# State-space stage: the diagonal products as two column tiles of 64 instead of one over 128 columns

## The chip, the cores and the metric

One of the eight cores of a Trainium2 chip runs the kernel. The metric is the device time of one execution in microseconds (us). Three runs of the kernel before gave 2584.29, 2584.89 and 2587.09 us; the median is 2584.89 us.

## The reference

The reference is one layer of a hybrid decoder over 1024 tokens of width 1024: token mixing (stick-breaking attention beside a Mamba-2 state-space branch), cross-attention into 256 memory tokens, and a SwiGLU feed-forward. What matters here is the state-space branch. It has 32 heads of width 64 in 4 groups of 8, and it works on chunks of 128 rows. Within a chunk each head's output has a diagonal term: a lower triangular 128 x 128 matrix (the group's C times B products, times the head's decay) applied to the head's 128 x 64 inputs.

```python
decay = jnp.exp(jnp.where(tril, a_cs[..., :, None] - a_cs[..., None, :], -jnp.inf))
cb = jnp.einsum('bclgn,bcsgn->bcgls', cc, bc)
y_diag = jnp.einsum('bcgls,bcgels,bcsgep->bclgep', cb, decay, xc)
...
return (y_diag + y_off).reshape(b, l, h, p)
```

Here `l` is the output row of the chunk, `s` the input row, `e` the head in its group and `p` the 64 columns of a head.

## The kernel before, in words

The kernel is one long program for five engines, and its stages follow each other: the input projection, the convolution and gates, attention, the state-space stage (from about 1080 to 1437 us of the span), the gated merge, cross-attention, the feed-forward. A scheduler that works from its own estimate of every instruction's duration writes the order on each engine; the text of the kernel gives the dependences, and some hand-set marks that keep one instruction behind another.

The state-space stage works on 32 pairs of a group and a chunk. For each pair it has these steps, which the scheduler lets overlap with those of other pairs:

- `prep` loads the inputs `xs` (128 rows x 512 columns: 8 heads of 64), makes the decay by a product on TensorE (L1048) and an exponential on ScalarE (L1049), and multiplies it by the C times B products on VectorE (L1050). The result is `seg`, 8 matrices of 128 x 128, one for each head, with the input row on the partitions and the output row along the free dimension.
- `states` carries the running state from chunk to chunk (TensorE L104 to L106 into `pst`, GpSimd L1072, VectorE L1073, then a split into a high and a low part, ScalarE L98 and VectorE L101).
- `outp` forms the output. GpSimd starts `y` with the skip term (L1089). The term of the earlier chunks comes from three matmuls into `po`, VectorE L1094 and GpSimd L1095. The diagonal term comes from **8 matmuls into `pd` (L1100)**, one for each head; their weights are `seg` of the head, their moving operand the head's columns of `xs`. VectorE adds `pd` to `y` (L1103) and multiplies by the gate (L1104). ScalarE makes the sum of squares (L1107), and the scaling follows (L1109).
- `flip` turns `y` by four transposes (L1122), and `branch` multiplies it with a weight matrix (the groups `mm<-oth,bw` of L104 to L106, which are most of the stage's matmuls). In the first quarter of the stage, matmuls of the memory's keys and values run between these steps.

The matmuls into `pd` are plain float32, not the rounded float32 kind (`fp32r`) that the others use. A float32 matmul shows as two passes, each with a weight load (engine PEld in the profile) and a matmul (PE): 32 pairs x 8 heads x 2 passes are the 512 records of L1100. The weights are 128 columns wide, so a pass writes all 128 partitions of `pd`. The moving operand is 96 columns and not 64, except for head 0: the loop goes from head 7 down to head 0, and each matmul also writes the 32 columns left of its own, which the next head's matmul writes again. `pd` has one buffer, so a pair's first matmul into it waits for the L1103 of the pair before.

Another matmul of the kernel, L406 at about 45 to 58 us, has weights of 64 columns only and writes partitions 0 to 63; it stands among others with 128.

Of the kernel before, what the change touches and what calls it, by code (L numbers as in the profile page):

```python
# [25 lines left out]
NH, HD = 16, 64  # L26
NG, GH = 4, 8
# [7 lines left out]
def hybrid_block(ctx, tc, a, out, dbg=None):  # L35
    nc = tc.nc
    V, A, G, T = nc.vector, nc.scalar, nc.gpsimd, nc.tensor
# [11 lines left out]
    def mk(pl, shape, dt, tag, bufs=None):  # L49
        uid[0] += 1  # L50
        kw = {} if bufs is None else {"bufs": bufs}
        return pl.tile(shape, dt, tag=tag, name=f"{tag}_{uid[0]}", **kw)
# [50 lines left out]
    def mm3(ps, sh, sl, mh, ml, start, stop):  # L103
        first = T.matmul(ps, sh, mh, start=start, stop=False)  # L104
        T.matmul(ps, sh, ml, start=False, stop=False)  # L105
        T.matmul(ps, sl, mh, start=False, stop=stop)  # L106
        return first
# [42 lines left out]
    def rstd_of(ms):  # L150
        r = mk(stats, [P, 1], F32, "rstd")
        G.tensor_scalar(r, ms, EPS, None, ALU.add)  # L152
        G.tensor_tensor(r, r, mhalf, ALU.pow)
        return r
# [94 lines left out]
    with ExitStack() as pa:  # L249
# [486 lines left out]
        with ExitStack() as p2:  # L736
# [17 lines left out]
            marks = []  # L754
# [174 lines left out]
            for m in range(NM):  # L929
                h, half = m // 2, m % 2  # L930
                hp, r = m // 4, m % 4
# [18 lines left out]
    with ExitStack() as p3:  # L950
# [11 lines left out]
        def bc(t, c, g, n=HD):  # L962
            return t[:, c, g * GH:(g + 1) * GH].unsqueeze(2).to_broadcast([P, GH, n])

        def v3(t, n=HD):
            return t.rearrange("p (h d) -> p h d", d=n)
# [114 lines left out]
        def outp(n):  # L1081
            g, c = divmod(n, NCH)
            d, gd = chk[n], grp[g]
            rows_ = slice(c * P, (c + 1) * P)
            seg, xs = d["seg"], d["xs"]
            zs = mk(t2, [P, HALF], F32, "s2")
            nc.sync.dma_start(zs, zs_d[rows_, g * HALF:(g + 1) * HALF])
            y = mk(t2, [P, HALF], F32, "s2")
            G.tensor_tensor(v3(y), v3(xs), dsk[:, g * GH:(g + 1) * GH].unsqueeze(2).to_broadcast([P, GH, HD]), ALU.mult)  # L1089
            if c > 0:  # L1090
                po = mk(ps, [P, HALF], F32, "po")
                mm3(po, d["ch"], d["cl"], *gd["st", c], True, True)
                yo = mk(t2, [P, HALF], F32, "s2")
                V.tensor_tensor(v3(yo), v3(po), bc(eam, c, g), ALU.mult)  # L1094
                G.tensor_tensor(y, y, yo, ALU.add)  # L1095

            pd = mk(ps, [P, HALF], F32, "pd")
            for h in range(GH - 1, -1, -1):
                hs = slice(max(0, h * HD - 32), (h + 1) * HD)
                ins = T.matmul(pd[:, hs], seg[:, h, :], xs[:, hs], start=True, stop=True)  # L1100
                if h == GH - 1:
                    marks.append(ins)
            V.tensor_tensor(y, y, pd, ALU.add)  # L1103
            V.tensor_tensor(y, y, zs, ALU.mult)  # L1104
            junk = mk(t2, [P, HALF], BF16, "junk", bufs=1)
            ms = mk(stats, [P, 1], F32, "ms")
            A.activation(junk, y, AF.Square, scale=float(HALF) ** -0.5, accum_out=ms)  # L1107

            A.activation(y, y, AF.Copy, scale=rstd_of(ms))  # L1109
            d["y"] = y  # L1110
# [56 lines left out]
        marks = []  # L1167
# [102 lines left out]
        for n in range(-AHEAD, NN + 2):  # L1270
            if AHEAD <= n + AHEAD < NN:
                prep(n + AHEAD)
            mem_work((n + AHEAD) * NQ / MEM_SPAN)
            for l in loads.pop(n, []):
                branch_load(*l)
            if todo and todo[0][0] <= n:
                todo.pop(0)[1]()
            if 0 <= n + 1 < NN:
                states(n + 1)
            mem_work((n + AHEAD + 0.33) * NQ / MEM_SPAN)  # L1280
            if 0 <= n < NN:
                outp(n)
            mem_work((n + AHEAD + 0.67) * NQ / MEM_SPAN)
            if todo and todo[0][0] <= n:
                todo.pop(0)[1]()
            if 0 <= n - 2 < NN:
                flip(n - 2)
                if (n - 2) % 4 == 3:
                    g, c = divmod(n - 2, NCH)
                    fs = list(range(KT)) if c == 3 else list(range(4, KT)) + list(range(4))  # L1290
                    todo += [(n + 2, lambda g=g, hf_=c // 4, f=f: branch(g, hf_, f)) for f in fs]
# [70 lines left out]
    marks = []  # L1362
# [506 lines left out]
```

## Time and profile before

| | |
|---|---|
| time, median of 3 runs | 2584.89 us (2584.29 to 2587.09) |
| profiled execution | span 2585.2 us, from its first to its last instruction (the profile gives no other time of it) |
| granted TensorE clock, mean | 0.990 |
| TensorE matmul / weight load busy | 2493.1 us (96%) / 2061.1 us (80%) |
| VectorE, ScalarE, GpSimd busy | 69%, 44%, 33% |
| the matmuls into `pd` | 512 passes, 1105.8 to 1432.6 us |

PE is TensorE's matmuls and PEld its weight loads, which run beside the matmuls; DVE is VectorE, ACT ScalarE, POOL GpSimd and SP the engine that issues DMAs. A row of the timeline gives the start in us, the duration in us, the engine, the source line, the operation, what it writes and reads, the shapes and how many follow each other; `128*64` or `128*128` ahead of the shapes is rows times columns of the weights in the array. A matmul's record begins when it comes to the head of the array and holds its wait for weights, if there is one.

### The profile page before, as it was taken

The page shows a single profiled execution, that of the slowest core. Times are in us where ns is not written, and L with a number is a line of the kernel's source. Part 1 is how long each engine was busy: PE and PEld are TensorE (multiplying, and loading weights), DVE is VectorE, ACT ScalarE, POOL GpSimd, SP SyncE. Part 2 cuts the span into 40 slices and gives each one's busy share as a digit, 9 for nine tenths or more (in the row PEclk, how much of TensorE's full clock was granted, in tenths as well). Part 3 has the DMA queues.
Part 4 walks back from the last instruction along what each step waited for, and adds up shares of the span by engine and source line. Part 5 has one row for each costly group of instructions (what it writes and reads, how often), then busy time and mean ns, then how long its engine had stood idle before and what let it go on. Part 6 is the DMA issues. An engine that isn't in the chain of part 4 may idle for free. (4 is left out here: it accounts for less than half of the span.)

```text
span 2585.2 us, 32334 instructions
## 1 busy us (share of the span) xinstructions
PE 2493.1 (96%) x11866; PEld 2061.1 (80%) x11866; DVE 1793.6 (69%) x2093; ACT 1130.1 (44%) x2020; POOL 842.2 (33%) x650
## 2 busy tenths in 40 slices
PE   7999999999999999999999999999999999999998
PEld 5788887887888778787888788887787888887876
DVE  7765777776578887687888664416459666666997
ACT  5333455555466655455554312314234333334343
POOL 3221654443111111244655050101114333323762
PEclk9999999999999999989999999999999999999999
DMA  7431433333543443355322462411232232224232
GB/s 245 155 121 58 151 117 103 109 106 91 141 107 98 118 104 90 111 180 175 104 90 81 153 238 74 130 49 50 94 113 70 76 96 74 90 90 163 98 131 98
DMA packets 255272, 293.44 MB, mean 114 GB/s; under 512 B 17024, under 2 KB 175241, under 8 KB 254987
## 3 DMA queue, kind: packets, MB, share of 16 engines
q1 hardware_dynamic: 255114, 291.40, 36.2%
q8 instruction: 93, 1.52, 0.2%
q14 instruction: 65, 0.52, 0.1%
HBM read 200.10 MB, written 74.45 MB: 106 GB/s over the span
## 5 line engine op out<-in xcount | busy, mean ns | idle before, releaser
L861 DVE TENSOR_TENSOR_SCAN n<-n,mask 128x128 f32<-128x128 f32 (+7 forms) x128 | 189.6, 1506 | 23.5 <-ACT n L860 22.2
L101 DVE TENSOR_TENSOR sw<-sf,sw 128x512 fp32r<-128x512 f32 x150 | 129.0, 872 | 67.0 <-ACT sw L98 66.7
L183 POOL TENSOR_TENSOR sf<-wr,wr 128x512 f32<-128x512 f32 x38 | 59.3, 1560 | 277.8 <-DMA wr<-in_w_gu_dram 138.3
L878 ACT ACTIVATE wth<-tr,mone 128x512 fp32r<-128x512 f32 x192 | 110.6, 584 | 83.0 <-PE tr L875 82.3
L98 ACT ACTIVATE sw<-sf 128x512 fp32r<-128x512 f32 x150 | 92.0, 626 | 109.1 <-PE mm L217 94.0
L879 DVE SCALAR_TENSOR_TENSOR wtl<-tr,wth 128x512 fp32r<-128x512 f32 x192 | 99.7, 544 | 50.6 <-ACT wth L878 50.6
L101 DVE TENSOR_TENSOR sw<-wr,sw 128x512 fp32r<-128x512 f32 x113 | 107.7, 955 | 27.6 <-ACT sw L98 27.5
L217 PE MATMUL mm<-h,sw 128*128 128x512 f32 x320 | 124.8, 391 | 1.8 <-DVE sw L101 1.8
L215 PE MATMUL mm<-h,sw 128*128 128x512 f32 x320 | 122.6, 391 | 2.9 <-ACT h L98 2.3
L216 PE MATMUL mm<-h,sw 128*128 128x512 f32 x320 | 125.1, 391 | 0.0
L104 PE MATMUL mm<-oth,bw 128*128 128x512 f32 (+1 forms) x320 | 122.5, 383 | 2.3 <-DVE a L1159 2.0
L98 ACT ACTIVATE sw<-wr 128x512 fp32r<-128x512 f32 x113 | 70.7, 628 | 120.9 <-PE mm L217 120.8
L106 PE MATMUL mm<-oth,bw 128*128 128x512 f32 (+1 forms) x320 | 120.0, 375 | 1.5 <-DVE bw L1146 1.5
L105 PE MATMUL mm<-otl,bw 128*128 128x512 f32 (+1 forms) x320 | 119.1, 372 | 0.0
L663 DVE SCALAR_TENSOR_TENSOR b<-b,prmT,b 128x1023 f32<-128x1023 f32 (+2 forms) x72 | 108.6, 1511 | 10.7 <-ACT b L661 10.0
L94 POOL TENSOR_SCALAR v<-va 128x512 fp32r<-128x512 f32 x16 | 20.6, 1291 | 285.4 <-PE av L888 165.8
L860 ACT ACTIVATE n<-sc 128x512 f32<-128x512 f32 (+1 forms) x192 | 88.6, 494 | 45.6 <-PE tr L875 28.8
L152 POOL TENSOR_SCALAR rstd<-ms 128x1 f32<-128x1 f32 x74 | 27.9, 376 | 242.3 <-ACT x L1380 111.5
L104 PE MATMUL p<-bw,h 128*128 128x512 f32 x256 | 99.4, 393 | 3.3 <-DVE x L1382 2.4
L106 PE MATMUL p<-bw,h 128*128 128x512 f32 x256 | 100.8, 394 | 0.0
L105 PE MATMUL p<-bw,h 128*128 128x512 f32 x256 | 100.4, 392 | 0.0
L185 POOL TENSOR_TENSOR sf<-wr 128x512 f32<-128x512 f32 x38 | 63.4, 1667 | 110.2 <-DVE sw L101 110.2
(607 smaller groups left out, 8033.1 us busy)
## 6 DMA issues: line engine op xcount, KB each, us to landing
wr<-in_w_gu_dram SPq DMA_DIRECT2D x80, 256.0 KB
wr<-in_w_in_dram SPq DMA_DIRECT2D x36, 512.0 KB
zr<-in_w_in_dram SPq DMA_DIRECT2D x28, 512.0 KB
gu_d<-t SPq DMA_DIRECT2D x44, 256.0 KB
wraw<-in_w_in_dram SPq DMA_DIRECT2D x20, 512.0 KB
zs_d<-zo SPq DMA_DIRECT2D x32, 256.0 KB
xs_d<-b SPq DMA_DIRECT2D x32, 256.0 KB
kl<-gt SPq DMA_DIRECT2D x64, 128.0 KB
```

The costliest lines, as they stand in the source:

```text
L98: A.activation(o, i, AF.Copy)
L101: eng.tensor_tensor(o, i, hi.bitcast(F32), ALU.subtract)
L104: first = T.matmul(ps, sh, mh, start=start, stop=False)
L105: T.matmul(ps, sh, ml, start=False, stop=False)
L106: T.matmul(ps, sl, mh, start=False, stop=stop)
L215: T.matmul(ps, w[0][:, k, :], bh, start=first and k == 0, stop=False, skip_group_check=True)
L216: T.matmul(ps, w[0][:, k, :], bl, start=False, stop=False, skip_group_check=True)
L217: ins = T.matmul(ps, w[1][:, k, :], bh, start=False, stop=last and k == 3, skip_group_check=True)
L663: V.scalar_tensor_tensor(acc[:, sh:], y[:, :S - sh], cw(3 - sh, f), acc[:, sh:], ALU.mult, ALU.add)
L861: V.tensor_tensor_scan(nt[:, 0:L][:, ::-1], nt[:, 0:L][:, ::-1], mask[:, S - L:][:, ::-1], 1.0, ALU.mult, ALU.max)
L878: A.activation(wh[:, t0 * P:], pt[:, t0 * P:], AF.Identity, bias=mone)
L879: V.scalar_tensor_tensor(wl[:, t0 * P:], pt[:, t0 * P:], -1.0, wh[:, t0 * P:].bitcast(F32), ALU.add, ALU.subtract)
```

## The change

The diagonal product of a head is cut in two along the output rows. One matmul has the weights for rows 0 to 63 (64 of the 128 columns of the head's `seg`) and writes partitions 0 to 63 of `pd`; a second has those for rows 64 to 127 and writes partitions 64 to 127. In the array these are two column tiles, of 128 rows by 64 columns each, at columns 0 and 64. Both have the same moving operand, the head's own 64 columns; the 32 columns more are gone. There are 16 matmuls for each pair in place of 8, or 1024 passes in place of 512, with weight loads of 64 columns in place of 128. The mark that keeps other work behind the first of these matmuls is set on the first half of head 7.

```diff
             pd = mk(ps, [P, HALF], F32, "pd")
             for h in range(GH - 1, -1, -1):
-                hs = slice(max(0, h * HD - 32), (h + 1) * HD)
-                ins = T.matmul(pd[:, hs], seg[:, h, :], xs[:, hs], start=True, stop=True)
-                if h == GH - 1:
-                    marks.append(ins)
+                hs = slice(h * HD, (h + 1) * HD)
+                for j in range(2):
+                    r = slice(j * HD, (j + 1) * HD)
+                    ins = T.matmul(pd[r, hs], seg[:, h, r], xs[:, hs], start=True, stop=True)
+                    if h == GH - 1 and j == 0:
+                        marks.append(ins)
             V.tensor_tensor(y, y, pd, ALU.add)
```

## The prediction

> **What bounds the kernel now.** I read the page's first lines, then the stage in which the changed matmuls stand, by stretches, then what TensorE waits for in it.
>
> ```profile
> span 2585.2 us, 32334 instructions
> PE 2493.1 (96%) x11866; PEld 2061.1 (80%) x11866; DVE 1793.6 (69%) x2093; ACT 1130.1 (44%) x2020; POOL 842.2 (33%) x650
> ```
>
> ```profile
> core 0: us, PE busy (x) PEld busy (x) DVE busy (x) ACT busy (x) POOL busy (x), PEclk, DMA share, GB/s
> 1105.00:1437.00 332.00, 320.48 (x1808) 274.59 (x1807) 273.25 (x333) 173.06 (x327) 174.00 (x167) 0.98 0.39 119
> ```
>
> ```profile
> PE pd L1100 <- DVE s L1103: 2.5, 2, 1.8
> PE dec L1048 <- ACT s L1049: 2.2, 3, 1.3
> PE dec L1048 <- DVE cb L1025: 1.6, 1, 1.6
> ```
>
> The second fence is the stretch of 332 us that holds all the changed matmuls. PE is busy for 320.5 of it, 97%; VectorE comes next with 273 us, 82%. The third fence has PE's longest waits there (us in total, times, longest): 2.5 us is the largest. So TensorE bounds this stage, and work taken off it or put on it changes the time nearly one for one, until VectorE's order catches up. A busy PE is not one at its peak, though; a short matmul may be waiting for its weights. So the next view is one run of the changed matmuls, first the matmuls and then the weight loads:
>
> ```profile
> 1207.54 0.40 PE L106 MATMUL mm<-oth,bw 128*128 128x512 f32 x1
> 1207.77 1.89 PE L1100 MATMUL pd<-s,s 128*128 128x96 f32 x16
> 1209.47 0.47 PE L104 MATMUL mm<-oth,bw 128*128 128x512 f32 x1
> 1209.79 0.39 PE L105 MATMUL mm<-otl,bw 128*128 128x512 f32 x1
> ```
>
> ```profile
> 1207.54 1.99 PEld L1100 LDWEIGHTS pd<-s,s 128*128 128x128 f32 x16
> 1209.45 0.19 PEld L104 LDWEIGHTS mm<-oth,bw 128*128 128x128 f32 x1
> 1209.56 0.19 PEld L105 LDWEIGHTS mm<-otl,bw 128*128 128x128 f32 x1
> ```
>
> The first load of the run starts at 1207.54, under the wide matmul ahead of it, and the second when the first pass starts, at 1207.77. From there to the load of the next wide matmul, at 1209.45, lie 15 more: 1.68 us / 15 = 0.112 us each, and the next pair of loads (1209.45, 1209.56) stands 0.11 apart too. Each load begins as soon as the one before is done. Is it the load that sets this pace, or the matmul? The durations say, in ns (minimum, median, maximum); the first row is the whole of L1100, the second the first pass of this run:
>
> ```profile
> L1100 PE MATMUL pd<-s,s x512: 218/275/422, 1105.8 to 1432.6; 128*128 128x96 f32 x149, 128*128 128x64 f32 x22
> L1100 PE MATMUL pd<-s,s x1: 244/244/244, 1207.8 to 1207.8; 128*128 128x96 f32 x1
> L1100 PEld LDWEIGHTS pd<-s,s x2: 187/188/188, 1207.5 to 1207.8; 128*128 128x128 f32 x2
> ```
>
> The first pass, whose weights lay ready, took 244 ns with 96 columns; the shortest of all, 218, I take as one with 64. The 26 ns between them over 32 columns are 0.81 ns a column: 64 columns stream in 52 ns, 96 in 78. Both are less than 112. **The runs are bound by their weight loads**, and the 32 columns that fall away are worth nothing.
>
> **The change part by part.** *The loads.* What does a load of 64 columns cost? L406 has such loads, among matmuls that start 0.23 us apart as here (rows below):
>
> ```profile
> L406 PEld LDWEIGHTS pdt<-b11h,wds x4: 133/134/135, 45.7 to 49.3; 128*64 128x64 f32 x4
> ```
>
> 134 ns against 187 to 188 for 128 columns: 53.5 ns less for 64 columns less. Of the load's record the part that sets the pace is 112 ns, so a load of 64 columns should allow a pace of 112 - 53.5 = 58 ns. The matmul of 64 columns streams in 52 ns, so the load still sets the pace. Half the load, twice as many: that is the whole trade, and it comes out slightly worse, since the fixed 5 ns a load (112 - 2 x 53.5) is paid twice.
>
> How many? The order in which the two built programs hold PE's instructions shows the passes of the 32 pairs in 47 runs before (some pairs are split by other matmuls) and in 50 after. In each run the first load lies under the wide matmul ahead, and the load of the wide matmul behind it, 112 ns, is paid in its place. Before: 512 x 0.112 = 57.3 us, whichever load it is. After: (1024 - 50) x 0.058 = 56.5 us, and 50 x 0.112 = 5.6 us for the wide loads, together 62.1 us. The difference is **+4.8 us**; at PE's 97% of the stretch, +4.6.
>
> The pace of two halves in turn, at columns 0 and 64, is the one price that no row shows: L406 uses the left half alone. Bounds from the nearest rows: 29 ns a pass if the two halves load wholly side by side (two passes each 58 ns), 112 ns if a narrow pass keeps the pace of a wide one. I take 58, since the rows for both halves of the pair (load 134, stream 52) give it without a new mechanism.
>
> *The passage between widths.* Ahead of and behind each run the array changes from tiles of 128 columns to tiles of 64 and back, 100 times. L406 does so before:
>
> ```profile
> 45.67 0.40 PE L216 MATMUL pv<-vl,b11h 128*128 128x512 f32 x1
> 45.90 0.39 PE L406 MATMUL pdt<-b11h,wds 128*64 128x512 f32 x1
> 46.13 0.39 PE L217 MATMUL pv<-vh,b11l 128*128 128x512 f32 x1
> 46.36 0.40 PE L215 MATMUL pv<-vh,b11h 128*128 128x512 f32 x1
> ```
>
> Starts are 0.23 us apart in all three steps, into the narrow tile, out of it, and between two wide ones. A passage costs nothing here, so I put nothing in the sum. A rule speaks against that: the Trainium skill, "TensorEngine Tiling (Array Packing)", section Key Properties, says that a change of the tiling mode drains TensorE. This trace does not agree for the left half; no row shows the right half. Its price is the second rival below.
>
> *The order.* The scheduler orders the stage anew. By the two orders PE, ACT, DVE, POOL and SP are the same until the stage starts. From there POOL moves 10 of 655 instructions (L1095 and L1055 past each other), SP 25 of 1021 (loads of `btm`, `bfm`, `zs` and `colrows` by a few places), ACT 82 of 1900, DVE 130 of 2095, all by a few places; PE shifts matmuls of `branch` against runs of `pd`, and a few dozen in the two projections after the merge; from the last third on it is as before. I cost that at nothing, with 4 us to either side: its cover is that PE works at 97%, and the largest single wait of PE above, 1.8 us, shows what one misplaced wait costs. If the cover is gone, the place to look is L1103: it waits for `pd`, and the next pair's first pass waits for it (the 2.5 us).
>
> *Sum.* 2585.2 + 4.6 = 2589.8 us by the span; the median of the runs shown stands 0.3 us under the span, so **2589.5 us**.
>
> **The rivals.**
>
> *The halves load side by side (faster).* One mechanism: a load for columns 64 to 127 starts while columns 0 to 63 still load or wait. At 29 ns the passes cost 974 x 0.029 + 5.6 = 33.8 us, 23.5 less than before. It decides from a pace under 53 ns ((57.3 - 5.6) / 974). For it: the halves share no columns and no weights. Against it: in both load fences a load starts only when the matmul ahead of it has begun, and the two passes of one half follow each other in the same columns, so only every second load has a neighbour in the other half. Not all of it would be won: PE would need 297 of VectorE's 273 us, and the chain of waits passes through other engines for long stretches here:
>
> ```profile
> 1378.93 1.74 POOL s L1095
> 1380.67 1.01 POOL s L1055
> 1381.70 0.64 ACT s2r L98
> 1382.37 1.52 DVE s2r L101
> ```
>
> I take two thirds: -15.5, or 2569.4 us; all of it would be 2561.4. The Trainium skill states it as a rule, on the same page and in the same section: different tiles can load weights and multiply in parallel. No row of this trace shows two tiles at work.
>
> *Each passage drains the array.* A wide matmul's record is 0.39 us and the next starts 0.23 after, so 0.16 us of it would be waited out. 100 passages are 16 us: 2589.5 + 16 = 2605.5 us. Against it stand the four rows of L406.
>
> *A narrow pass does not reach 58 ns.* The sequencer now issues a load and a matmul at twice the rate. No stretch shows a pace under 112. Half way, 85 ns, is 974 x 0.085 + 5.6 = 88.4 us, +31: 2616 us; at 112 it is 114.7 us, +57: 2642 us.
>
> **How the numbers follow.** Loads in turn at 58 ns: 0.45, from 2583 to 2596 (with the order's 4 us to either side, and 2 ns of pace, 2 us). Side by side: 0.30, from 2561 to 2582. Drain: 0.13, from 2600 to 2610. Slower pace: 0.12, from 2597 to 2642. A measurement of this kernel tells about 0.2%, 5.2 us, from no change, so "same" is 2579.7 to 2590.1. Faster: nearly all of side by side and little of the first, 0.31. Same: half of the first case and a remnant of the second, 0.24. Slower: the other half of the first, 0.20, and both slower rivals, 0.25: 0.45 together. The range 2567 to 2610 leaves out the lower end of side by side (0.08) and most of the slower pace (0.10). Since cases of both signs count, the likeliest one's own range is 2583 to 2596.
>
> **What would show it.** Right: in a run of `pd`, 64-column loads of about 134 ns, 58 ns apart, and a run of 32 passes of about 1.9 us to the next wide matmul, where 16 took 1.70; the first narrow pass 0.23 us after the start of the wide one ahead. Side by side: a run near 1 us, two loads that start within some 10 ns, and new waits of PE for DVE or POOL in the stage. Drain: a gap of 0.16 us or more at both ends of each run, and an even pace within. Slower pace: even spacing of 80 ns and more inside the runs. The stage from 1080 us on should hold all of the difference; if it lies in the projections after it, the order made it and the sum above is wrong.

## The result, and the profile after

The change takes 2577.34 us (median of 6 runs, 2575.45 to 2581.21) against 2585.02 us for the kernel before: **0.997 of its time, 95% interval 0.996 to 0.998**. That is 7.7 us faster. Two later sets gave 2576.01 us (0.9968, 0.9957 to 0.9979) and 2575.76 us (0.9959, 0.9947 to 0.9972). The forecast was 2589.5 us, 4.6 us slower than the runs it went by; the time lies inside the range of 2567 to 2610 us, but it moved the other way.

The same run of the diagonal passes as in the prediction, in the profile of the change, matmuls first and then weight loads:

```profile
1209.47 0.39 PE L106 MATMUL mm<-oth,bw 128*128 128x512 f32 x1
1209.79 1.15 PE L1102 MATMUL pd<-s,s 128*64 128x64 f32 x32
1210.87 0.50 PE L104 MATMUL mm<-oth,bw 128*128 128x512 f32 x1
1211.20 0.39 PE L105 MATMUL mm<-otl,bw 128*128 128x512 f32 x1
```

```profile
1209.24 0.19 PEld L106 LDWEIGHTS mm<-oth,bw 128*128 128x128 f32 x1
1209.78 1.01 PEld L1102 LDWEIGHTS pd<-s,s 128*64 128x64 f32 x32 [0.35 <-DVE state L1073]
1210.87 0.19 PEld L104 LDWEIGHTS mm<-oth,bw 128*128 128x128 f32 x1
1210.97 0.19 PEld L105 LDWEIGHTS mm<-otl,bw 128*128 128x128 f32 x1
```

Two things are to be seen. The 32 passes take 1.08 us to the start of the next wide matmul, where 16 took 1.70. And the first narrow load does not lie under the wide matmul ahead of it, as every load did before: it starts 0.31 us after that matmul (1209.47 to 1209.78), with weight loading idle for 0.35 us. The same run in a stretch of 0.1 us at its start (counts, then minimum, median and maximum in ns), and the waits of the whole kernel's stretch from 1092 to 1472 us:

```profile
1209.78 0.14 PEld L1102 LDWEIGHTS pd<-s,s 128*64 128x64 f32 x2 [0.35 <-DVE state L1073]
```

```profile
L1102 PEld LDWEIGHTS pd<-s,s x2: 133/133/133, 1209.8 to 1209.8; 128*64 128x64 f32 x2
```

```profile
PEld pd L1102 <- issue: 10.3, 31, 0.4
```

Two loads of 133 ns each are done within 0.14 us, since the second starts 7 ns after the first: the left and the right half load side by side. (Records of loads in one half overlap too, but those loads start 58 ns apart, as a run below shows.) The third fence has the other thing again: 31 times, at the head of a run, weight loading stands idle for 0.33 us on average with nothing in the profile to wait for ("issue"). The kernel before has no such row at L1100. For the run shown the profile names VectorE's L1073, but that had ended at 1209.61, and the gap is as long as the others. What the load does go by is the matmul ahead: at 49 of the 50 runs' heads the first narrow load starts 0.07 us before the end that the profile gives for that matmul (a modelled end), whether its record lasts 0.27 or 0.50 us. So the load waits until the matmul ahead is nearly out of the array; before, it started as that matmul started.

Now the stage as a whole, from its first decay matmul to the end of its last branch matmul, first before and then after:

```profile
1091.00:1479.00 388.00, 370.06 (x2012) 313.02 (x2012) 313.67 (x390) 195.71 (x364) 181.57 (x175) 0.97 0.42 130
```

```profile
1092.00:1472.00 380.00, 358.53 (x2525) 287.20 (x2525) 311.63 (x392) 196.85 (x364) 183.41 (x175) 0.98 0.44 133
```

TensorE's busy time falls by 11.5 us, its idle time rises from 17.9 to 21.5 us, and the stage is 8.0 us shorter. The spans of the two profiles differ by 10.3 us, so 2.3 us lie outside the stage; single profiles scatter by as much there.

### The profile page after: what moved, and what is told of

It reads as the page before. It is cut to its first block, busy times and chain, and to the rows that moved or that the text cites. A ratio compares the mean times of both kernels' runs of the same rounds, so it can differ in the third digit from the quotient of the medians.

```text
span 2574.9 us, 33360 instructions
## 1 busy us (share of the span) xinstructions
PE 2479.3 (96%) x12378; PEld 2032.9 (79%) x12378; DVE 1786.7 (69%) x2093; ACT 1130.3 (44%) x2020; POOL 843.0 (33%) x650
## 5 line engine op out<-in xcount | busy, mean ns | idle before, releaser
L861 DVE TENSOR_TENSOR_SCAN n<-n,mask 128x128 f32<-128x128 f32 (+7 forms) x128 | 189.5, 1507 | 23.5 <-ACT n L860 20.2
```

The lines of the kernel that those rows point to most:

```text
L861: V.tensor_tensor_scan(nt[:, 0:L][:, ::-1], nt[:, 0:L][:, ::-1], mask[:, S - L:][:, ::-1], 1.0, ALU.mult, ALU.max)
```

## The experiments

**64 columns, the weights as before.** What are the 32 columns more worth, and what is a new order of the stage worth? The run was meant for both questions.

```diff
-                hs = slice(max(0, h * HD - 32), (h + 1) * HD)
+                hs = slice(h * HD, (h + 1) * HD)
```

> The kernel before, with the moving operand of the diagonal matmuls cut from 96 columns to 64; the weights stay 128 columns wide. The scheduler orders the stage anew, as it does for the change. Theory (the change gains because two narrow loads run side by side, and loses at each passage between widths): the wide loads still set the pace, a whole run of 16 passes stays 1.70 us to the next wide matmul, and the time stays within 4 us of before. Rival (the gain came from the new order of the stage): the time moves by something like the -7.7 us of the change with the runs unchanged.

Measured: 2584.42 us, ratio 0.9998 (0.9989 to 1.0007). A run, in the timeline:

```profile
1218.02 1.89 PE L1100 MATMUL pd<-s,s 128*128 128x64 f32 x16
1219.72 0.48 PE L104 MATMUL mm<-oth,bw 128*128 128x512 f32 x1
```

16 passes take 1.70 us, as with 96 columns. The loads of 128 columns set the pace, and the 32 columns more were worth nothing. On the order the run says nothing: by the traces all matmuls of TensorE, all instructions of ACT, DVE and POOL and SP's DMA issues follow each other exactly as in the kernel before, with the same 47 runs of passes. The expectation that the scheduler orders anew was wrong here; the next run bears on the order.

**Half after half.** The same loads and the same passages, without a neighbour in the other half.

```diff
-            for h in range(GH - 1, -1, -1):
-                hs = slice(h * HD, (h + 1) * HD)
-                for j in range(2):
+            for j in range(2):
+                for h in range(GH - 1, -1, -1):
+                    hs = slice(h * HD, (h + 1) * HD)
```

> The change with its two loops swapped: all 8 heads' left halves, then all 8 right halves. The same 16 matmuls, so the same loads and passages in number, but neighbours are in the same columns except once in a run. Theory (the overlap needs a neighbour in the other half): loads 58 ns apart, a whole run of 32 passes about 1.9 us plus the passages, the stage some 28 us longer than with the change, about 2600 to 2605 us. Rival (the array keeps several narrow loads under way whatever their columns, or looks far ahead in its queue): a run near 1.1 us and about 2577 us.

Measured: 2587.78 us, ratio 1.0009 (1.0000 to 1.0018). The timeline and the stage:

```profile
1210.10 1.90 PE L1102 MATMUL pd<-s,s 128*64 128x64 f32 x32
1211.92 0.50 PE L104 MATMUL mm<-oth,bw 128*128 128x512 f32 x1
```

```profile
1091.50:1483.50 392.00, 379.21 (x2522) 309.30 (x2523) 314.73 (x389) 197.09 (x363) 182.10 (x175) 0.98 0.42 128
```

A run takes 1.82 us. Within a half the weight loads start 58 ns apart; only where the right half follows the left, the one place with neighbours in different halves, do a few run side by side. So the overlap needs a neighbour in the other half, and the rival falls. The time was forecast 12 to 17 us too high: TensorE is busy 20.7 us longer than with the change (379.2 against 358.5), but its idle time falls from 21.5 to 12.8 us, and 12 us are left in the stage, 10 in the time. Work put on TensorE shortens its waits for the other engines.

This run also bears on the order. By the traces it has nearly that of the change: POOL's is the same, and on PE, ACT and DVE together 22 instructions stand elsewhere (a run of passes counted as one). So with the order the same, and 50 runs in both, the pace of the passes makes the 10 us. What the new order is worth against the old one can only be estimated: on a straight line between this run (TensorE busy for 379.2 us, idle for 12.8) and the change (358.5 and 21.5), TensorE would be idle for 16.6 us at the 370.1 us busy of the kernel before, which is idle for 17.9. That leaves about 1 us for the order, too little to tell from nothing.

**Wide, then the left half; wide, then the right half.** Two runs, with 8 narrow matmuls added to each pair that write one half again (their work is extra); the wide ones ahead of them have 64 columns. The lines added for the left half:

```diff
+            for h in range(GH - 1, -1, -1):
+                hs = slice(h * HD, (h + 1) * HD)
+                r = slice(0 * HD, 1 * HD)
+                T.matmul(pd[r, hs], seg[:, h, r], xs[:, hs], start=True, stop=True)
```

> The diagonal product as before at 64 moving columns, and after it, in the same pair, 8 matmuls more that write the left half (rows 0 to 63) again with 64-column weights. Work is added: 16 narrow passes for each pair. It shows the passage between wide and narrow weights for the left half alone, in plain float32. Theory A (any narrow tile drains the array): the first narrow load starts only about 0.15 us after the last wide pass has left the head of the array, as in the change. Theory B (only the right half's place makes the mode, as L406 suggests): the first narrow load starts under the last wide pass, no gap. Inside the narrow part both expect 58 ns a pass. Time by B about +30 us (32 x 16 x 0.058), by A some 8 more.

> As the run with the left half, but the 8 added matmuls write the right half (rows 64 to 127) again. Both theories expect the gap of about 0.15 us at the passage here; the two runs differ by some 8 us if only the right half drains, and by nothing if any narrow tile does.

Measured, one run each: 2613.03 us (left) and 2612.82 us (right). The weight loads around a narrow run, of the left half and then of the right:

```profile
1255.88 0.42 PEld L1100 LDWEIGHTS pd<-s,s 128*128 128x128 f32 x3
1256.37 1.01 PEld L1106 LDWEIGHTS pd<-s,s 128*64 128x64 f32 x16
1257.44 0.19 PEld L104 LDWEIGHTS mm<-oth,bw 128*128 128x128 f32 x1
```

```profile
1256.76 1.53 PEld L1100 LDWEIGHTS pd<-s,s 128*128 128x128 f32 x13
1258.36 1.01 PEld L1106 LDWEIGHTS pd<-s,s 128*64 128x64 f32 x16
1259.44 0.19 PEld L104 LDWEIGHTS mm<-oth,bw 128*128 128x128 f32 x1
```

The last of the three wide loads ends at 1255.88 + 0.42 = 1256.30, so it began at 1256.11; the narrow load follows 0.26 us later in place of 0.11. Of the 16 narrow loads, 58 ns apart, the last begins at 1257.24; the wide one follows after 0.20 in place of 0.06. Each passage costs about 0.15 us, in and out, and the right half is the same (1258.10 to 1258.36). Theory A holds: it is not the right half's place. As in the change, the load starts 0.07 us before the end of the matmul ahead, here in both directions. The times are below what either theory gave: the profile with the left half has 32.6 us more of busy TensorE than the kernel before (2525.7 against 2493.1), and its span is 26.1 us longer. As with half after half, not all work put on TensorE reaches the end.

**The left half in rounded float32.** Why, then, did L406 pass for nothing? It is of the other type, and its matmuls are long.

```diff
                 mm3(po, d["ch"], d["cl"], *gd["st", c], True, True)
+                sth, stl = gd["st", c]
+                for h in range(GH):
+                    hs = slice(h * HD, (h + 1) * HD)
+                    mm3(po[0:HD, hs], d["ch"][:, 0:HD], d["cl"][:, 0:HD], sth[:, hs], stl[:, hs], True, True)
```

> The kernel before, with work added to the state term: after the three 512-column matmuls into po, 24 matmuls write its left half (rows 0 to 63) again with weights of 64 columns, in rounded float32 and with 64 moving columns each. Theory A (the array drains where narrow and wide weights meet, whatever the type): a gap of some 0.15 us or more between the wide matmul ahead and the first narrow load, as the added narrow passes in plain float32 showed. Theory B (the rounded type has no such passage, as L406 showed with 512 moving columns): the first narrow load starts with the wide matmul ahead of it, within 10 ns. No claim on the time.

Measured, one run: 2621.82 us. The last wide matmul ahead of such a run, then the first and the last loads:

```profile
1248.54 0.39 PE L106 MATMUL po<-sth,cl 128*128 128x512 f32 x1
```

```profile
1248.32 0.19 PEld L106 LDWEIGHTS po<-sth,cl 128*128 128x128 f32 x1
1248.54 0.13 PEld L104 LDWEIGHTS po<-sth,ch 128*64 128x64 f32 x1
...
1250.05 0.14 PEld L106 LDWEIGHTS po<-sth,cl 128*64 128x64 f32 x1
1250.11 0.41 PEld L1104 LDWEIGHTS pd<-s,s 128*128 128x128 f32 x3
```

The first narrow load starts with the wide matmul ahead (1248.54), and the wide load behind follows the last narrow one after 0.06 us. No passage is paid: theory B. With short matmuls too, the rounded type in the left half goes in and out of the wide ones for nothing, and plain float32 does not. What in the array makes the difference between the types stays open; the right half was not tried in the rounded type.

**Whole runs.** The change, with TensorE's order held so that 35 runs are left of 50. `behind` queues what a block emits behind the named matmuls; the same is done for the matmuls of the memory's keys and values.

```diff
-                T.matmul(pe, f4["keys"][:, cs], cr[:, hs, :], start=True, stop=True)
+                with behind(prun):
+                    latest[:] = [T.matmul(pe, f4["keys"][:, cs], cr[:, hs, :], start=True, stop=True)]
...
-            for h in range(GH - 1, -1, -1):
+            with behind(latest):
+                for h in range(GH - 1, -1, -1):
...
+            prun[:] = [ins]
```

> The change, with the order of TensorE held so that the matmuls of the decay and of the memory's keys and values no longer stand inside a run of the diagonal passes: 35 runs in place of 50, the same passes. Theory (a run costs some 0.26 us for its two passages, and about two thirds of TensorE's gain reaches the end): 15 x 0.26 = 3.9 us less on TensorE, 2 to 3 us less in time, about 2575 us. Rival (passages are hidden by the waits for other engines, or the held order costs as much as it saves): 2577 us or more.

> The change itself, unaltered, beside the others on the same chip. Theory: 2577 us, 0.997 of before, as first measured; a whole run of 32 passes 1.08 us to the next wide matmul. No rival: it is the yardstick for the other runs of this set.

> The change with whole runs, again, beside the change on the same chip, since the first comparison left their intervals overlapping. Theory: 2 to 3 us below the change. Rival: no difference that five rounds can tell.

> The change itself as the yardstick of this set: 2576 to 2577.5 us, 0.997 of before.

Measured: whole runs 2573.39 us (0.9957, 0.9943 to 0.9970) beside the change with 2576.01 (0.9968, 0.9957 to 0.9979); again 2574.81 (0.9959, 0.9946 to 0.9973) beside the change with 2575.76 (0.9959, 0.9947 to 0.9972). Both medians are lower, by 2.6 and 1.0 us, and the intervals overlap both times. Inconclusive: if fewer passages pay here, it is by less than these runs can tell. The stage of the first of the two shows the saving on TensorE: 354.8 us busy against 358.0 in the profile of the change beside it, 3.2 us for 15 runs where 3.9 were forecast.

```profile
1091.00:1469.00 378.00, 354.77 (x2524) 286.28 (x2524) 308.35 (x388) 196.08 (x362) 183.97 (x175) 0.96 0.43 131
```

**Quarters.** Four column tiles of 32, first in the scheduler's order, then with the order held as above.

```diff
-                for j in range(2):
-                    r = slice(j * HD, (j + 1) * HD)
+                for j in range(4):
+                    r = slice(j * 32, (j + 1) * 32)
```

> The change with four column tiles of 32 in place of two of 64: 32 matmuls, 64 passes a pair. A load of 32 columns should set a pace of 32 ns in its tile (27 + 5), a stream of 64 columns 52 to 56. Theory (tiles work side by side, each bound by the slower of its load and its stream): 64 passes / 4 tiles x 56 ns = 0.9 us and the passages, a run of 1.05 us against 1.08, the time equal to that of the change within 3 us. Rival (about 29 ns a pass is what the sequencer can issue): a run of 64 x 29 ns = 1.9 us and a time near 2588 us, as with half after half.

> The four tiles of 32 columns with the order of TensorE held as in the run with whole runs (34 runs of the diagonal passes in place of 49). Theory (the quarters' runs are as short as the halves', and their time was given back as waits in the order that the scheduler made for them): with the order held the waits of TensorE in the stage fall from 34 us to about 23 us and the time is that of the halves with the held order, 2574 us within 3. Rival (quarters cost something outside their runs, in issue or in fetching twice the instructions): 2583 us or more with the order held too.

Measured: 2588.21 us (1.0015, 1.0006 to 1.0024), and 2584.96 us (0.9994, 0.9986 to 1.0003) with the order held. A run and the stage, of the first:

```profile
1208.20 1.10 PE L1102 MATMUL pd<-s,s 128*32 128x64 f32 x64
1209.24 0.50 PE L104 MATMUL mm<-oth,bw 128*128 128x512 f32 x1
```

```profile
1087.00:1479.00 392.00, 358.22 (x3545) 284.44 (x3545) 313.26 (x389) 195.35 (x363) 179.22 (x175) 0.97 0.42 128
```

64 passes take 1.04 us, as the theory said: four tiles side by side, and no floor of 29 ns a pass. Within a tile the loads start 56 ns apart, near the 52 ns in which 64 columns stream and far from the 32 ns estimated for the load, so the streams seem to bind. But the time is that of the kernel before or worse: TensorE is as busy as with the halves (358.2 and 358.5 us), and idle for 34 us of the stage against 21.5. I put that down to the scheduler's order; with the order held the waits should have gone, and they did not (TensorE's idle time there is 34 us again, counted from the first decay matmul to the last branch matmul, and the time 10 us over the halves). The theory's forecast fell, and the time is in the rival's range, 2583 us or more. The order is still not excluded: the hold keeps some matmuls out of the runs and leaves the rest to the scheduler, and by the traces 75 instructions of DVE and 53 of ACT stand elsewhere than in the whole runs of the halves. Why a run that is as short makes TensorE wait for longer stays open.

## Why the prediction was wrong

**The pace of two halves in turn** is the step that failed: "the one price that no row shows", bounded by 29 and 112 ns, for which 58 was taken "without a new mechanism". It is 28 to 29: (1.01 - 0.14) / 31 by the row of the weight loads, (1.08 - 0.15 for the passage out) / 32 by the matmuls. Half after half shows that 58 was right for neighbours in one half, and that only the neighbour in the other half makes the difference. The bounds held it; the choice between them was wrong. The argument against side by side (a load starts only when the matmul ahead has begun) was read off matmuls that all used the same columns, and so could say nothing of two sets of columns. "Each load begins as soon as the one before is done" was a misreading too, though the pace holds: records of 187 ns that start 112 ns apart overlap. The rule of the Trainium skill, "TensorEngine Tiling (Array Packing)", section Key Properties, that tiles load and multiply in parallel, agrees with the two loads of 133 ns that are done within 0.14 us.

**The passage between widths** failed too, the other way: nothing was put for it, and it costs about 0.26 us a run. Without it a run, from the wide matmul ahead to the second one behind, would be 0.23 + 31 x 0.029 + 0.112 + 0.23 = 1.47 us; the rows show 1209.47 to 1211.20, or 1.73. (The same sum for the kernel before, with 15 x 0.112, gives 2.25, and its rows show 2.25.) The row it was read from, L406, was of another type; the run with rounded float32 shows that it was a true row, and of the wrong kind of matmul. The rule of the Trainium skill, in the same section, that a change of the tiling mode drains TensorE agrees with the plain float32 runs, where the load waits for the matmul ahead, and not with the rounded ones.

**The rivals were taken one at a time.** Side by side and drain stood with 0.30 and 0.13, as if one excluded the other. Both came, with opposite signs. In the sum's own terms: 974 passes x (0.029 - 0.058) = -28.2 us, 50 runs x 0.26 = +13.0 us, and the +4.8 of the sum: -10.4 us. TensorE's busy time in the stage fell by 11.5. That the time lies in the range given for side by side, 2561 to 2582, is in part luck: its own sum was 2569.4 us, and the passages, which it did not have, brought the time up from there.

**What reached the end.** Two thirds were forecast for the faster case: 8.0 us of the 11.5 are seen in the stage, 0.7. But the main sum had used 0.97, from TensorE's busy share; half after half shows that too much: of 20.7 us put back on TensorE, 12 came through in the stage. The quarters show that a share cannot be taken for granted at all: with TensorE's busy time as low as with the halves, nothing reached the end. (A slip without weight: two thirds of the rival's 23.5 us are 15.7, not 15.5.)

**What was right.** The loads bound the wide runs; the 96 columns were worth nothing; a load of 64 columns sets a pace of 58 ns in its half; the number of runs and loads. That the new order costs nothing fits the estimate of about 1 us from half after half, but no run had the new order with the old matmuls.

## What to carry to other kernels

Where short matmuls follow each other and their weight loads set the pace, cutting the output rows into column tiles shortens the runs if neighbours in the queue lie in different tiles; here the same matmuls tile after tile lost all of the gain. Count the passages between tile widths as a term of its own, measured on the same data type. Shorter runs are not yet a shorter kernel: the quarters had them and gained nothing. And before a run is read as a test of the order, compare the order in its trace. When a price lies between bounds far apart, and a row seems to settle it, ask whether the row's instruction differs in any respect that the price could hang on.

## What the runs showed of the hardware that was not expected

- Two weight loads of 64 columns, for columns 0 to 63 and 64 to 127, run side by side: 28 to 29 ns a pass in turn, 58 ns in one half.
- Between wide weights and narrow ones of plain float32, the next load waits until 0.07 us before the end of the matmul ahead, some 0.15 us in and 0.15 out; narrow ones of rounded float32 in the left half do not make it wait, with 64 or 512 moving columns.
- Four tiles of 32 columns pass at 16 ns (1.04 us for 64 passes, the passage out included).
